# A two-layer hybrid block on one core: output weights split during the projections and kept in DRAM

## The chip, the cores and the metric

The kernel runs on one core of one Trainium2 chip. The metric is the device time of the program in microseconds. A core has TensorE (PE, its weight loads PEld), VectorE (DVE), ScalarE (ACT), GpSimd (POOL), and SyncE (SP), which here issues all DMAs. Each engine runs its own queue of instructions in order.

## What is computed

Two layers over 2048 tokens of width 1024 and 256 context tokens, in float32. The core of a layer, cut from the reference:

```
hx = rmsnorm(x, g_pre) * (1 + scale[:, None]) + shift[:, None]
q, k, v, ga, uf, gf, zc, bc, cc, gc = split_cols(hx @ w_in, PROJ_SIZES)
...
a = window_attention(q, k, v, kc, vc, sink_b)
f = fourier_mix(uf, w_fourier)
s = short_conv_mix(zc, bc, cc, conv_w, conv_b)
y = gated_merge(a, ga, f, gf, s, gc, w_out)
x_new = x + gate[:, None] * rmsnorm(y, g_post)
```

`gated_merge` concatenates `a * silu(ga)` (512 wide), `f * silu(gf)` (256) and `s * silu(gc)` (256) and multiplies by `w_out`, 1024 x 1024 per layer. The context tokens go through the same layer with the context attending to itself; the second layer computes only their keys and values.

## The kernel before

**Number format.** Each float32 operand of a product is split into a high part (rounded to the matmul's format, `fp32r`) and a low part (the rest), and a product is three matmuls: high by high, high by low, low by high. `split` (L76) does this: one engine rounds (L79, L81 or L83 for VectorE, ScalarE, GpSimd), one subtracts (L85 or L87). These lines are those of all splits, so the names of the tiles tell them apart.

**Stages of a layer.** First the projections: `half(l, 0)` takes tokens 0 to 1023 and the context, `half(l, 1)` tokens 1024 to 2047, in chunks of 512 tokens. The normalised input of a chunk, `hx0` or `hx1`, is one pair of tiles `big` (high, low), 128 x 8 x 512 each, from a pool of four. One column block of 128 columns times one chunk is `proj` (L304): 24 matmuls into an `acc` of PSUM, three for each k; `tick` (L118) stands behind each k and advances the generators in `fill` by a rate, so that side work is written into the order between matmuls. Weights come as `wr` (512 KB) and are split to `wh`, `wl`. In half 0 the last stages are the convolution projections (J_CV, with a fill of its own) and a pair of attention gates (J_GA 2 and 3, `sg`, stored to `gas` in DRAM). Half 1 begins with the two Fourier gates (`gf`), the K projection and then V (`accb`).

In layer 0 the input of a chunk is read as `xT` (two loads of 1 MB), and `pt_post` (L275) makes the eight k-slices of `hx`: VectorE `ht<-xT` (L288), ScalarE the high part (L289), VectorE the low (L290). Layer 1's modulation is computed on the side, by products on VectorE (L185) with weights `wmt` of 512 KB. In layer 0 the convolution stage of half 0 also carries `tab_gen` (L598): nine pieces of the Fourier table are loaded (`tr`), split on ScalarE and VectorE (`th`) and stored to `ftd` in DRAM.

Then `phase2(l)`, the attention and the output product, over blocks of 128 tokens (in layer 0 the two context blocks first). Each block has two steps, one for each key head. In a step the generators A (scores and softmax of this block: `sp`, `nm`, `pt`, `es`, `rv`), B (transposes `tp` of the probabilities, split to `ph` and `pl`, product with the values into `op`) and C (output product `yp`) are advanced in the order of the letters in a string; in the first three steps C is instead a gate projection left over from half 1 (`lt`). B also loads the block's gates `gat` and Fourier rows `fct`, and rounds the latter into `hfh` and `hfl` on GpSimd. V and W are `wout_gen(l, 0)` and `wout_gen(l, 1)`: each loads four chunks of 512 KB of its half of the output weights and splits each chunk into a pair of `big`, VectorE and ScalarE (in one case GpSimd) by tables WV and WE. V runs in steps 0 and 1, W in steps 2 and 3. `behind` only says after which instructions of an engine's queue they stand. The order on each engine's queue is fixed when the program is built; a scheduler places the instructions, so a DMA that is written early can stand late.

## Time and profile before

| | us |
|---|---|
| median of 3 runs | 2040.29 (2035.42 to 2041.83) |
| profiled execution, time | 2034.59 |
| profiled execution, span | 2032.8 |
| TensorE busy in it | 1967.9 (97%) |
| VectorE, ScalarE, GpSimd busy | 1245.6, 847.7, 746.4 |

The mean granted clock of TensorE is 0.992 of full. The core reads 214.37 MB of HBM and writes 75.38 MB. The attention of layer 0 begins at about 614 us and of layer 1 at about 1600 us. A busy TensorE is not TensorE at its peak, but where it is not busy the end of the program waits. In a window row the columns are the window, its length, then for PE, PEld, DVE, ACT and POOL the busy time with the number of instructions, then the granted clock, the share of the DMA engines, and GB/s. In a timeline row they are start, duration, engine, line, operation, and in brackets how long the engine sat idle before and who released it.

### The profile page before, as it was taken

To read this page: it belongs to the slowest core of one execution; us is meant where nothing else is said; L and a number is where in the kernel's file an instruction comes from. 1 tells how busy PE (TensorE), PEld (TensorE's weight loads), DVE (VectorE), ACT (ScalarE), POOL (GpSimd) and SP (SyncE) were. 2 spreads that over 40 slices of the span, in tenths; PEclk is the share of its full clock that TensorE was granted. 3 is DMA by queue.
4 is the path that set the end of the run, shared out by engine and by line. 5 is a ranking of instruction groups with operands and counts; after the bars stand their busy time and mean duration, and the time that the engine had idled before them with its cause. 6 is when DMAs were issued, how large, how long until landed. Compare 5 with 4: busy or idle time off the path is not lost.

```text
span 2032.8 us, 28494 instructions
## 1 busy us (share of the span) xinstructions
PE 1967.9 (97%) x10232; PEld 1665.3 (82%) x10232; DVE 1245.6 (61%) x2240; ACT 847.7 (42%) x1742; POOL 746.4 (37%) x965
## 2 busy tenths in 40 slices
PE   6999999999999899999999999999999999999998
PEld 2898788797887788888887988889888778888886
DVE  7824674748535677777778424142764377777775
ACT  6532212213224566666666312131222356666663
POOL 4322232215233444444455333242333434444442
PEclk8999999999999999999999999999999999999999
DMA  7684663566566244444333533134655734444321
GB/s 299 225 254 135 195 201 103 184 200 181 169 186 202 90 112 114 114 113 116 126 116 127 179 89 104 63 112 125 179 178 158 206 113 114 116 115 116 105 63 42
DMA packets 187038, 291.63 MB, mean 143 GB/s; under 512 B 15608, under 2 KB 119696, under 8 KB 185872
## 3 DMA queue, kind: packets, MB, share of 16 engines
q1 hardware_dynamic: 186896, 289.80, 46.8%
q8 instruction: 81, 1.33, 0.3%
q14 instruction: 61, 0.50, 0.1%
HBM read 214.37 MB, written 75.38 MB: 143 GB/s over the span
## 4 chain that ended last, share of the span: by engine, by line
PE 76%; DVE 8%; DMA 7%; POOL 4%; issue 3%; ACT 2%; SPq 1%; DVEq 0%; POOLq 0%; ACTq 0%
PE acc L302 10%; PE acc L300 10%; PE acc L301 10%; PE tp L1159 7%; PE yp L1210 6%; PE yp L1208 6%; PE yp L1209 6%; PE sp L1111 4%; PE op L1173 4%; PE op L1172 3%; PE sp L1108 3%; PE accb L398 2%; PE accb L399 2%; PE accb L400 2%; DMA wmt<-in_wmodt 2%
## 5 line engine op out<-in xcount | busy, mean ns | idle before, releaser
L300 PE MATMUL acc<-big,wh 128*128 128x512 f32 x1152 | 454.9, 395 | 1.6 <-ACT wh L81 1.6
L302 PE MATMUL acc<-big,wl 128*128 128x512 f32 x1152 | 451.0, 391 | 1.9 <-DVE wl L85 1.9
L301 PE MATMUL acc<-big,wh 128*128 128x512 f32 x1152 | 450.7, 391 | 0.6 <-DVE big L290 0.6
L87 POOL TENSOR_TENSOR wl<-wr,wh 128x1024 fp32r<-128x1024 f32 x63 | 158.0, 2508 | 384.5 <-ACT wh L81 275.5
L85 DVE TENSOR_TENSOR pl<-tp,ph 128x512 fp32r<-128x512 f32 x320 | 218.9, 687 | 104.8 <-ACT ph L81 100.4
L1121 ACT ACTIVATE pt<-pt,nm 128x640 f32<-128x640 f32 (+2 forms) x272 | 216.3, 795 | 130.5 <-DVE nm L1118 130.0
L302 PEld LDWEIGHTS acc<-big,wl 128*128 128x128 f32 x1152 | 217.3, 189 | 48.4 <-DVE wl L85 2.8
L300 PEld LDWEIGHTS acc<-big,wh 128*128 128x128 f32 x1152 | 217.7, 189 | 43.9 <-ACT wh L81 2.0
L301 PEld LDWEIGHTS acc<-big,wh 128*128 128x128 f32 x1152 | 217.6, 189 | 43.4 <-DVE big L290 1.0
L81 ACT ACTIVATE ph<-tp 128x512 fp32r<-128x512 f32 x320 | 188.7, 592 | 132.0 <-PE tp L1159 122.5
L1118 DVE CUSTOM_DVE_ANT_0 pt<-sp,mask,nsink 128x640 f32<-128x640 f32 (+2 forms) x256 | 213.3, 841 | 19.8 <-PE sp L1108 14.1
L1133 POOL TENSOR_SCALAR pt<-pt,rv 128x640 f32<-128x640 f32 (+2 forms) x272 | 212.1, 799 | 27.0 <-DVE rv L1131 25.8
L1159 PE MATMUL tp<-ident,pt 128*128 128x128 f32 x1280 | 195.5, 273 | 9.2 <-POOL pt L1133 8.5
L1159 PEld LDWEIGHTS tp<-ident,pt 128*128 128x128 f32 x1280 | 158.9, 140 | 55.4 <-POOL pt L1133 14.1
L1111 PE MATMUL sp<-kseg,qt 128*128 128x384 f32 (+1 forms) x512 | 128.5, 331 | 0.0
L345 POOL TENSOR_TENSOR rs<-rs,sinT 128x512 f32<-128x512 f32 x40 | 67.2, 1682 | 161.1 <-DVE rs L343 156.3
L1208 PE MATMUL yp<-big,hfh 128*128 128x512 f32 x272 | 118.5, 435 | 1.0 <-POOL hfh L83 1.0
L1126 POOL TENSOR_TENSOR es<-nm,nsink 128x4 f32<-128x4 f32 x68 | 14.5, 213 | 282.8 <-DVE nm L1118 282.8
L1208 PE MATMUL yp<-big,hah 128*128 128x512 f32 x272 | 117.1, 431 | 0.1
L1108 PE MATMUL sp<-kctx,qt 128*128 128x256 f32 x544 | 113.9, 291 | 2.9 <-DVE nm L1118 2.1
L1108 PEld LDWEIGHTS sp<-kctx,qt 128*128 128x128 f32 x544 | 95.4, 189 | 16.5 <-DVE nm L1118 3.6
L1210 PE MATMUL yp<-big,hfl 128*128 128x512 f32 x272 | 107.8, 396 | 0.5 <-POOL hfl L87 0.4
(380 smaller groups left out, 3805.4 us busy)
## 6 DMA issues: line engine op xcount, KB each, us to landing
wr<-in_wina SPq DMA_DIRECT2D x76, 512.0 KB, 3.7
qt<-qs SPq DMA_DIRECT2D x34, 512.0 KB, 4.7
wmt<-in_wmodt SPq DMA_DIRECT2D x32, 512.0 KB, 4.3
ftb<-ftd SPq DMA_DIRECT2D x36, 384.0 KB, 4.1
xt<-in_x SPq DMA_DIRECT2D x26, 512.0 KB, 5.9
kseg<-ks SPq DMA_DIRECT2D x24, 512.0 KB, 8.4
xt<-x SPq DMA_DIRECT2D x24, 512.0 KB, 4.5
gat<-gas SPq DMA_DIRECT2D x34, 256.0 KB, 3.1
```

The costliest lines, as they stand in the source:

```text
L85: self.last_v = nc.vector.tensor_tensor(lo, src, f(hi), op=ALU.subtract)
L300: nc.tensor.matmul(a, wh[:, k, :], hi[:, k, :n], start=(k == 0), stop=False)
L301: nc.tensor.matmul(a, wh[:, k, :], lo[:, k, :n], start=False, stop=False)
L302: nc.tensor.matmul(a, wl[:, k, :], hi[:, k, :n], start=False, stop=(k == KT - 1))
L1108: nc.tensor.matmul(sp[:, 256:512], B.q[:, h, :], self.kctx[:, kv, x, :], start=(x == 0), stop=(x == 1))
L1111: nc.tensor.matmul(sp[:, 512:512 + nl], B.q[:, h, :], B.seg[:, kv, x, B.k0:B.k0 + nl], start=(x == 0), stop=(x == 1))
L1118: self.last_m = nc.vector.tensor_tensor_reduce(d, x, m, scale=-0.125, scalar=self.nsink[:, h:h + 1], op0=ALU.add, op1=ALU.min, accum_out=n ...
L1121: self.last_x = nc.scalar.activation(pt, pt, AF.Exp, bias=nm[:, hh:hh + 1], scale=-1.0, accum_out=sm[:, hh:hh + 1])
L1133: self.last_p = nc.gpsimd.tensor_scalar(B.pts[kv][g], B.pts[kv][g], rv[:, g:g + 1], 1.0, op0=ALU.mult, op1=ALU.mult)
L1159: nc.tensor.transpose(tp[:, hh * 128:(hh + 1) * 128], pts[hh][:, t * 128:(t + 1) * 128], self.ident)
L1208: nc.tensor.matmul(yp, hh, wh[:, k, :], start=(i == 0), stop=False)
L1210: nc.tensor.matmul(yp, hl, wh[:, k, :], start=False, stop=(i == KT - 1))
```

## The change

Three things change.

1. `wout_split(l)` is new. It runs in the fill of the convolution stage of half 0, in both layers (in layer 0 behind `tab_gen`). For each of 16 pieces it loads 128 x 512 raw output weights (256 KB), rounds them on ScalarE, subtracts on VectorE, and stores both parts (512 KB) to a DRAM tensor `wos[l]`. The rate of this fill goes from 0.12 to 0.27 in layer 0 and is 0.26 in layer 1.
2. `wout_gen` issues only loads: eight of 512 KB for each half of the weights, high and low parts straight into `big`. The splits in the attention are gone. The strings of steps 2 and 3 place W differently; step 3 has one string for both layers.
3. For the first block of a layer the Fourier rows are rounded behind the last key tile of its second step in place of the second.

The layout of the input `wout` follows. The code before `half` loses five lines, so L85 becomes L80, L190 becomes L185, and so on.

```diff
-WE_A = ["vv", "av", "vv", "av"]
-WE_B = ["vv", "vp", "vv", "av"]
-WV_A = ["vv", "av", "vv", "vv"]
-WV_B = ["vv", "av", "vv", "av"]
-ORDER_2 = "bAACACACWCCBCBCWBCBABBCBBB"
-ORDER_3A = "bAAWCCBcBCABBAWCBBCBBCcACBCBB"
-ORDER_3B = "bAAWCCBcBCABBAWCBBCBBCcACBCBB"
+ORDER_2 = "bAACACACCCBCBCBCBABBCBBB"
+ORDER_3 = "bWAAWCCBcBCABBAWCBBCBBCcACBWCBB"
...
-RT = 0.6, 0.594, 0.616, 0.1, 0.13, 0.12, 0.49
+RT = 0.6, 0.594, 0.616, 0.1, 0.13, (0.27, 0.26), 0.49
...
     def tab_gen(self, p):
         nc = self.nc
         for k in range(9):
-            raw = p.tile([128, 384], F32, name="tr", tag="tr")
+            raw = p.tile([128, CH], F32, name="tr", tag="tr")[:, :384]
             nc.sync.dma_start(raw, self.I["ftab"][:, k])
             yield
-            h = p.tile([128, 2, 384], F32R, name="th", tag="th")
+            h = p.tile([128, 2, CH], F32R, name="th", tag="th")[:, :, :384]
             self.split(h[:, 0], h[:, 1], raw, "a", "v")
             nc.sync.dma_start(self.ftd[k], f(h))
             yield
...
             if half == 0:
                 cvp = self.pool(e3, f"cv{l}{half}", bufs=1)
             fills = [ff] if half else []
-            if l == 0 and half == 0:
-                mp = self.pool(e3, "mp", bufs=1)
-                fills.append(self.start_fill(self.tab_gen(mp), RT[5]))
+            if half == 0:
+                mp = self.pool(e3, f"mp{l}", bufs=1)
+
+                def rest():
+                    if l == 0:
+                        yield from self.tab_gen(mp)
+                    yield from self.wout_split(l, mp)
+                fills.append(self.start_fill(rest(), RT[5][l]))
             for ct in range(2):
                 segs = [("m", HALF), ("c", NCTX)] if (half == 0 and not last_l) else [("m", HALF)]
                 tl = {}
...
             end = t == nkt - 1
             nc.tensor.matmul(op, vv, hl[t][0], start=(t == 0), stop=False)
             nc.tensor.matmul(op, vv, hl[t][1], start=False, stop=end)
-            if kv == 1 and t == 1:
+            if kv == 1 and t == (1 if B is not self.Bs[0] else nkt - 1):
                 B.hf = (p.tile([128, 4, 128], F32R, name="hfh", tag="hfh", bufs=1),
                         p.tile([128, 4, 128], F32R, name="hfl", tag="hfl", bufs=1))
                 self.split(*B.hf, B.fc, "p", "p")
...
         return self.vtiles[b]
 
     def wout_gen(self, l, n):
-        wh, wl = self.big(), self.big()
-        self.wout.append((wh, wl))
-        for c in range(4):
+        W = [self.big(), self.big()]
+        self.wout.append(W)
+        for c in (2, 3, 0, 1):
             with self.behind(self.last_st):
-                raw = self.wraw(self.I["wout"][l, n * 4 + c])
-            sl = slice(c * 128, (c + 1) * 128)
-            with self.behind(self.last_x, self.last_m):
-                self.split(wh[:, :, sl], wl[:, :, sl], raw, *((WV_A, WE_A), (WV_B, WE_B))[l][n][c])
+                for t, src in zip(W, self.wos[l][n]):
+                    self.nc.sync.dma_start(f(t[:, 2 * c:2 * c + 2]), src[:, 2 * c:2 * c + 2])
             yield
+
+    def wout_split(self, l, p):
+        nc = self.nc
+        for n in range(2):
+            for k in range(KT):
+                raw = p.tile([128, CH], F32, name="tr", tag="tr")
+                nc.sync.dma_start(raw, self.I["wout"][l, n, :, k])
+                yield
+                h = p.tile([128, 2, CH], F32R, name="th", tag="th")
+                self.split(h[:, 0], h[:, 1], raw, "a", "v")
+                nc.sync.dma_start(self.wos[l][n, :, :, k].rearrange("x p c -> p x c"), f(h))
+                yield
 
     def ctx_gen(self, l, before):
         nc = self.nc
...
                         drain(V)
                         W = self.wout_gen(l, 1)
                     gens["V"], gens["W"] = V, W
-                    emit(gens, (ORDER_0, ORDER_1, ORDER_2, (ORDER_3A, ORDER_3B)[l])[s])
+                    emit(gens, (ORDER_0, ORDER_1, ORDER_2, ORDER_3)[s])
                     if s == 3:
                         drain(W)
                 else:
...
             c1 = dp.tile([NCTX, D], F32, name="c1")
             self.x = [I["x"], x1, self.out]
             self.ctx = [I["ctx"], c1]
+            self.wos = [dp.tile([2, 2, 128, KT, CH], F32, name=f"wos{l}") for l in range(DEPTH)]
             self.gsl = [dp.tile([128, 2, TOK], F32, name=f"gs_{l}") for l in range(DEPTH)]
             for l in range(DEPTH):
                 self.qs = dp.tile([128, 8, TOK], F32, name=f"qs{l}")
...
     a["winb"] = ac(w_in[:, :, np.r_[640:768, 1280:1536]]).reshape(DEPTH, KT, 128, 384)
     rows = np.concatenate(pairs + [np.arange(512, 1024)])
     wo = w_out[:, rows, :]
-    a["wout"] = ac(wo.reshape(DEPTH, KT, 128, 8, 128).transpose(0, 3, 2, 1, 4)).reshape(DEPTH, 8, 128, KT * 128)
+    a["wout"] = ac(wo.reshape(DEPTH, KT, 128, 2, CH).transpose(0, 3, 2, 1, 4))
     a["sink"] = ac(sink)
     wf = np.zeros((DEPTH, 2, 128, 128), np.float32)
     for g in range(4):
```

The first place is the queue of SP in layer 0, from the end of half 0's convolution stage. `gas<-sg` are the stores of the gates, `xT` the input of half 1's second chunk, `wmt` the modulation weights of layer 1, `tr`, `th` and `wos` the load, the split tile and the store of a piece. Before:

```order
L373 DMA fs_88<-cy 128x256
L783 DMA gas_87<-sg 128x512
L266 DMA xT_3045<-in_xT 128x4x512
L266 DMA xT_3046<-in_xT 128x4x512
L190 DMA wmt<-in_wmodt 128x1024
L783 DMA gas_87<-sg 128x512 x2
```

After:

```order
L1274 DMA wos_81<-th 128x2x512
L1270 DMA tr<-in_wout 128x512
L778 DMA gas_89<-sg 128x512
L778 DMA gas_89<-sg 128x256
L377 DMA wr<-in_winb 128x2x384
L1274 DMA wos_81<-th 128x2x512
L185 DMA wmt<-in_wmodt 128x1024 x2
L261 DMA xT_3143<-in_xT 128x4x512
L261 DMA xT_3144<-in_xT 128x4x512
```

`xT` stood behind the first of the six gate stores; it now stands behind all six, the last store of a piece and two `wmt`.

The second is VectorE right after it, in layer 0, where the second chunk's `hx1` is made; `ISA jk,mo` are products for layer 1's modulation. Before:

```order
L185 ISA jk,mo_1511<-wmt,sb 128x1024
L185 ISA mo_1511 128x1
L181 TENSOR_SCALAR G_1512<-mo_1511,gp_1507 128x2
L185 ISA jk,mo_1511<-wmt,sb 128x1024
L185 ISA mo_1511 128x1
L288 SCALAR_TENSOR_TENSOR ht<-xT_3045,G_153,rb_3049 128x512 x2
L180 TENSOR_SCALAR mo_1511<-mo_1511,bm_1505 128x2
L290 SCALAR_TENSOR_TENSOR big<-ht,mo_152,big 128x512
```

After:

```order
L80 TENSOR_TENSOR th<-tr,th 128x512
L180 ISA jk,mo_1513<-wmt,sb 128x1024
L180 ISA mo_1513 128x1
L180 ISA jk,mo_1513<-wmt,sb 128x1024
L180 ISA mo_1513 128x1
L175 TENSOR_SCALAR mo_1513<-mo_1513,bm_1507 128x2
L180 ISA jk,mo_1513<-wmt,sb 128x1024
L180 ISA mo_1513 128x1
L176 TENSOR_SCALAR G_1514<-mo_1513,gp_1509 128x2
L180 ISA jk,mo_1513<-wmt,sb 128x1024
L180 ISA mo_1513 128x1
L283 SCALAR_TENSOR_TENSOR ht<-xT_3143,G_155,rb_3147 128x512
```

Between the last piece and the first `ht` stand four such products now, and five more among the `ht` and `big` that follow.

The third is GpSimd at the start of layer 0's attention, with `-` for before and `+` for after:

```order
 L1133 TENSOR_SCALAR pt<-pt,rv 128x256 x4
-L87 TENSOR_TENSOR hfl<-fct,hfh 128x512
 L1126 TENSOR_TENSOR es<-nm,nsink 128x4
 L1128 TENSOR_TENSOR es<-es,sm 128x4
 L1133 TENSOR_SCALAR pt<-pt,rv 128x256 x4
+L78 TENSOR_SCALAR hfh<-fct 128x512
+L82 TENSOR_TENSOR hfl<-fct,hfh 128x512
```

`hfh` stood ahead of the first of these `pt`. Both roundings stand behind the second group now.

## Rows read from the trace of the kernel before

**Rows 1.** The page, busy time of each engine.

```profile
PE 1967.9 (97%) x10232; PEld 1665.3 (82%) x10232; DVE 1245.6 (61%) x2240; ACT 847.7 (42%) x1742; POOL 746.4 (37%) x965
```

**Rows 2.** Windows of the attention's starts, of half 0, and of two half-clock stretches.

```profile
core 0: us, PE busy (x) PEld busy (x) DVE busy (x) ACT busy (x) POOL busy (x), PEclk, DMA share, GB/s
614.00:670.00 56.00, 49.73 (x239) 38.47 (x238) 33.91 (x72) 26.71 (x65) 17.23 (x28) 1.00 0.56 184
670.00:720.00 50.00, 47.46 (x259) 39.45 (x259) 35.35 (x70) 27.53 (x65) 23.34 (x43) 1.00 0.40 116
720.00:816.00 96.00, 96.00 (x538) 82.29 (x538) 73.68 (x140) 58.74 (x132) 41.46 (x82) 1.00 0.41 112
1594.00:1710.00 116.00, 108.57 (x576) 90.06 (x575) 81.81 (x147) 63.50 (x138) 43.93 (x69) 0.99 0.50 144
235.00:290.00 55.00, 50.31 (x246) 42.56 (x245) 43.40 (x74) 9.85 (x18) 13.21 (x6) 0.94 0.71 233
290.00:345.00 55.00, 55.00 (x295) 47.60 (x294) 24.18 (x41) 7.44 (x13) 17.20 (x7) 1.00 0.25 87
239.70:246.60 6.90, 5.91 (x15) 4.66 (x16) 4.19 (x13) 1.74 (x3) 1.53 (x1) 0.51 0.70 263
1656.30:1659.70 3.40, 3.40 (x11) 2.82 (x10) 2.15 (x5) 3.21 (x6) 0.00 (x0) 0.50 0.02 5
```

**Rows 3.** TensorE's waits, 614 to 705 us, then 1594 to 1662 us.

```profile
PE tp L1159 <- POOL pt L1133: 5.6, 7, 1.7
...
PE op L1173 <- DVE pl L85: 2.8, 2, 2.2
```

**Rows 4.** Groups by line and form, VectorE, 614 to 672 us.

```profile
L85 DVE TENSOR_TENSOR big<-wr,big 128x1024 fp32r<-128x1024 f32 x8 | 10.2, 1284 | 0.2
```

**Rows 5.** Timeline of VectorE, layer 1's start.

```profile
1635.01 1.21 DVE L85 TENSOR_TENSOR big<-wr,big 128x1024 fp32r<-128x1024 f32 x1
...
1638.93 1.27 DVE L85 TENSOR_TENSOR pl<-tp,ph 128x512 fp32r<-128x512 f32 x2
```

**Rows 6.** Timeline of GpSimd, layer 0's start.

```profile
631.79 3.74 POOL L1133 TENSOR_SCALAR pt<-pt,rv 128x256 f32<-128x256 f32 x4
635.50 2.24 POOL L87 TENSOR_TENSOR hfl<-fct,hfh 128x512 fp32r<-128x512 f32 x1
...
639.53 2.33 POOL L1133 TENSOR_SCALAR pt<-pt,rv 128x256 f32<-128x256 f32 x4 [1.12 <-DVE rv L1131]
```

**Rows 7.** The page, costliest groups: the splits of a 128 x 512 tile.

```profile
L85 DVE TENSOR_TENSOR pl<-tp,ph 128x512 fp32r<-128x512 f32 x320 | 218.9, 687 | 104.8 <-ACT ph L81 100.4
...
L81 ACT ACTIVATE ph<-tp 128x512 fp32r<-128x512 f32 x320 | 188.7, 592 | 132.0 <-PE tp L1159 122.5
```

**Rows 8.** The tile `tr`, 190 to 300 us.

```profile
L81 ACT ACTIVATE th<-tr x8: 513/525/527, 230.1 to 282.4; 128x384 fp32r<-128x384 f32 x8
...
DMA to landing us min/median/max: 2.7/3.1/5.2
```

**Rows 9.** The tile `xT`, 340 to 400 us.

```profile
L288 DVE SCALAR_TENSOR_TENSOR ht<-xT,G,rb x8: 734/740/742, 369.6 to 382.7; 128x512 f32<-128x512 f32 x8
L266 SPq DMA_DIRECT2D xT<-in_xT x2: 384/442/500, 347.0 to 347.4; - x2
...
DMA to landing us min/median/max: 6.8/8.4/9.9
```

**Rows 10.** DMA issues, 340 to 400 us.

```profile
wmt<-in_wmodt SPq DMA_DIRECT2D x6, 512.0 KB, 4.2
```

**Rows 11.** Timeline of TensorE, start of half 1.

```profile
365.80 0.39 PE L300 MATMUL acc<-big,wh 128*128 128x512 f32 x1
...
385.39 0.50 PE L301 MATMUL acc<-big,wh 128*128 128x512 f32 x1 [0.58 <-DVE big L290]
...
402.29 0.34 PE L398 MATMUL accb<-wbh,big 128*128 128x384 f32 x1
```

**Rows 12.** Timeline of VectorE, start of half 1.

```profile
367.19 1.21 DVE L185 CUSTOM_DVE_ANT_0 jk<-wmt,sb 128x1024 bf16<-128x1024 f32 x1
```

## Prediction

> **What bounds the kernel now.** I read the page first: of a 2032.8 us span TensorE is busy 1967.9 us, 97% [rows 1]. No other engine passes 62%, so time can come only from the 65 us in which TensorE is not busy, or from making it wait more. The profiled execution took 2034.59 us, 1.8 us more than its span; the median of the three runs is 2040.29, so I make the sum against 2034.6 and add 5.7 us to carry it to the median.
>
> Next I cut the span into stretches around the places the change touches. The reader is to see that the attention is full in steady state (layer 0, 720 to 816 us: 96.00 of 96) and not at its start: in layer 0 49.73 of 56 us while the weights are split, 47.46 of 50 right after; in layer 1 108.57 of 116, and 3.4 us more at half clock behind the last stall (a granted clock of 0.50, that is 1.2 GHz of 2.4) [rows 2]. So 6.3, 2.5 and 7.4 us of idle TensorE, and 1.7 us of lost clock. This is what the change can give at first hand.
>
> Then the waits. At layer 0's start TensorE waits 5.6 us, in seven pieces, for `pt` of GpSimd; at layer 1's start 2.8 us for `pl` of VectorE [rows 3]. The question is whether the work on the output weights makes these late.
>
> **Part 1, the splits that leave the attention.** In layer 0 VectorE spends 10.2 us on eight subtractions of weights [rows 4], beside five roundings on it and three on ScalarE; layer 1 has much the same. Their cost is not their busy time, since both engines have idle time there, but their place in a queue that runs in order. The timeline of VectorE in layer 1 shows it: the subtraction of a weight stands at 1635.01 us, with its cast before it and `lt` after it, ahead of the `pl` that TensorE waits for, which starts only at 1638.93 [rows 5]. That is the longest wait, 2.2 us, of the 2.8. The same queue order stands behind the late row maxima and, through them, behind the late `pt`.
>
> **Part 2, the rounding of the first block's Fourier rows.** On GpSimd `hfh` waits for its load with `pt` behind it; then `hfl` takes 2.24 us and the next block's sums stand behind that [rows 6]. The change puts both behind the second group of `pt`, so the next `pt` no longer stand behind a load and two roundings.
>
> A row against a rule: the four `pt` at 631.79 took 3.74 us, and the four at 639.53 took 2.33 [rows 6]; beside the first VectorE worked on a subtraction. The Trainium skill (SBUF — State Buffer, Who interferes with whom) says that a VectorE instruction with two inputs in SBUF contends with a GpSimd instruction that reads SBUF. By that rule the 1.4 us come back with the subtractions gone, and the same contention appears in half 0, between the new subtractions and the GpSimd weight splits; the trace agrees as far as these two rows go. Without that rule layer 0 gives 1.4 us less.
>
> What goes: in layer 0 the 6.3 us, less a short wait on a gate's evacuation that stays, so 6; in layer 1 7.4 + 1.7 = 9.1, less the like and a rest of the half clock, so 8: **−14**. Not counted are the 2.5 us of 670 to 720 in layer 0, where no weight is being split any more. Bounds: −18 if all of it goes with them, 6.3 + 2.5 + 7.4 + 1.7; and −5 if only half of the waits of rows 3 (8.4 us) and of the lost clock go, because the next engine is late for the rest. I take −14 since a split, or `hfl`, stands ahead of the late instruction in each gap I followed back.
>
> **Part 3, the loads in the attention.** Four MB of raw weights per layer become eight MB, in sixteen loads of 512 KB. The busiest stretch of the rows moves 263 GB/s [rows 2]; 8 MB at that rate are 32 us, and the half that the first output product reads (4 MB, loaded first) 16 us, 25 with the other loads between them. That product starts near 655 us, some forty after the loads. SP issues five of them ahead of `gat` and `fct`, so `fct` lands some 10 us later; its rounding has been put later too. I cost this at 0, with up to 4 us if `fct` or the next `qt` is late: the upper bound of what the wait for `fct` could put back.
>
> **Part 4, the splits and stores in half 0.** Sixteen pieces per layer: a 256 KB load, a rounding on ScalarE, a subtraction on VectorE, a 512 KB store. A tile of this shape takes ScalarE 592 ns and VectorE 687 [rows 7]. The narrower pieces of the table, with loads of 3.1 us, run in the same way now, eight of them from 230 to 283 us, and TensorE waits for none [rows 8]. Busy time: 16 × 1.3 = 20 us per layer on two engines that from 290 to 345 us are busy 24.18 and 7.44 of 55 us while TensorE is full [rows 2]. Cost 0, bound +3.
>
> **Part 5, what the pieces push back.** The 9 + 16 pieces of layer 0 fill the whole convolution stage and run into the gate projections behind it. On SP the load of the next half's second chunk (`xT`, two of 1 MB) now stands behind the last store and two `wmt` loads. Before, it was issued at 347.0 and landed in 6.8 to 9.9 us, a good 12 us ahead of its first use at 369.6; the last tile was ready at 385.3, and TensorE already waited for it there [rows 9, 11]. This cover is used up. I place the issue: the store of the last context gate, whose projection ends where the next begins, at 365.8, precedes it [rows 11], with five more DMAs at some 0.4 us each, so 368.5. The two `wmt` land 4.2 us later, and four modulation products of 1.2 us stand ahead on VectorE [rows 10, 12]: 377.5; `xT` lands at 375 to 378. From there eight `ht` and eight `big` of 0.74 and five products, 18 us, to 395.5. TensorE, which goes through both Fourier-gate projections in step with these tiles, has then one k of them and two K projections left. From the wait at 385.39 to `accb` at 402.29 there are 74 matmuls, 0.228 us each [rows 11]; 48 for K and 6 for the last k are 12.3 us: 408, against 402.3. So **+6**. Bounds: 0, if the tiles come no later than now, and +12, if the last piece waits for its own load and store one after the other and `xT` is issued at 373.
>
> **Sum:** −14 + 6 + 0 + 0 = −8: 2034.6 → 2026.6 profiled, **2032** as a median. 0.3%, about what a measurement of this kernel can tell from no change, is 6.1 us.
>
> **The rivals.**
>
> *The starts stay as they are.* The 2.5 us of 670 to 720 have no split beside them, so a start may stall because its blocks change size, with another engine late in its turn. Then the attention gives −5, half 1 takes 6: 2036 profiled, 2041 on the median. For it: those stalls exist. Against: the timeline of rows 5.
>
> *The chain of pieces becomes the bound (slower).* Load, ScalarE, VectorE and store have one buffer each, and the order on each engine is fixed, so a late piece holds up the evacuations and weight splits behind it. From 230 to 365 us there are 135 us; nine narrow pieces of at most 0.5 + 0.7 + 3.1 us and 0.4 to issue, 4.7 in all, leave 93 for sixteen wide ones, 5.8 us each. My estimate of a wide cycle, from the rows of tile and load, is 0.6 + 0.7 + 3.1 + 0.5 = 4.9 us. It decides from 6 us: a table load took up to 5.2 us, with 233 GB/s moved in 235 to 290 [rows 2, 8]. At 7 us the last store comes 19 us late (16 × 1.2) and everything of part 5 with it: −14 + 6 + 19 = +11, so 2046 profiled, 2051 as a median.
>
> *No cost in half 1.* If `xT` is early enough, the whole −14 stands: 2020.6 profiled, 2026 on the median. Against it stands the order on SP.
>
> *The clock falls in the new wait.* TensorE would run in step with the tiles for some 18 us at little over half its work. At 239.7 to 246.6 us, after a long wait, the granted clock was 0.51 of full, that is 1.2 GHz, for 6.9 us [rows 2]: 3.4 us of work lost. The Trainium skill (TensorE: Matmul & The Clock Gate, HAM oscillation — how this bites in real kernels) describes a clock that falls again in each gap between bursts. By that rule the K projections would start at half clock and the loss be 6 + 3.4: −4.6, 2030 profiled, 2036 as a median. The trace bears out one fall after one long wait, and one of 3.4 us in layer 1's start.
>
> *The change does not do what it says.* The order of instructions shows splits and roundings moved, so I give this nothing.
>
> **How the numbers follow.** Forecast (net −5 to −12) 0.43; no cost in half 1 0.12; clock 0.15; the starts stay 0.18; chain the bound 0.12. Of the forecast's cases about three quarters lie beyond −6.1, of the clock's a third, and all of the third rival: faster 0.5. The starts-stay case and the rest of the forecast and clock give same 0.37. The chain, and a little of the starts-stay case with 12 us in half 1, give slower 0.13. The range reaches from −18 with nothing given back (2022), and a little below for the spread of the runs, to +6 (2046), which leaves out the worse half of the chain: 2020 to 2046.
>
> **What would show it.** Right: no wait for `pl` or `pt` behind a `big` at the starts, TensorE busy about 55 of 56 and 115 of 116 us in the two stretches; `xT` issued about 368 and the first `accb` of half 1 about 408. Wrong: stalls of the same sum at both starts with another releaser; the first `accb` at 402 or past 415; waits of ScalarE on `tr` that TensorE shares in half 0.

## The result, and the profile after

The changed kernel is slower by 0.6%: a median of 2052.1 us (2049.31 to 2053.13, 4 runs) against 2039.74 for the kernel before on the same chip, a ratio of 1.006 [1.0041, 1.008]. The profiled execution took 2053.13 us, its span is 2051.3, 18.5 longer than before. The medians differ by 12.4 only: the profiled execution of the kernel before lies 5.2 us under its median, this one 1.0 above. The page's first row:

```profile
PE 1974.7 (96%) x10232; PEld 1670.6 (81%) x10232; DVE 1246.2 (61%) x2247; ACT 859.8 (42%) x1768; POOL 731.8 (36%) x964
```

TensorE has the same number of matmuls as before [rows 1]. Of the 18.5 us 6.8 are longer busy time in them, and 11.7 are waiting. To find where, I set the start of the same matmul in both traces side by side:

| before, us | after is later by | what lies in between |
|---|---|---|
| 87 | 1.7 | the start, which the change does not touch: clock |
| 327 | 1.5 | |
| 350 | 12.9 | layer 0, half 0, convolution stage |
| 388 | 27.0 | first Fourier-gate projections of half 1 |
| 408 | 33.5 | the rest of them, into the K projections |
| 610 | 33.5 | |
| 670 to 1050 | 24.8 | start of layer 0's attention: −8.7 |
| 1455 | 25.8 | layer 1's half 0 |
| 1500 to 1600 | 29.5 | layer 1's Fourier transform |
| 1676 to the end | 18.5 | start of layer 1's attention: −11.0 |

So the attention gave more than forecast (−19.7), and layer 0's projections took back 32. The windows of the changed kernel (window, its length, busy time and count of each engine, granted clock, DMA share, GB/s):

```profile
core 0: us, PE busy (x) PEld busy (x) DVE busy (x) ACT busy (x) POOL busy (x), PEclk, DMA share, GB/s
647.50:694.80 47.30, 46.78 (x239) 38.92 (x239) 21.18 (x60) 23.36 (x62) 12.73 (x28) 1.00 0.80 268
694.80:744.80 50.00, 47.59 (x259) 39.30 (x259) 35.37 (x70) 27.53 (x65) 23.36 (x43) 1.00 0.51 152
1623.50:1728.50 105.00, 104.74 (x576) 89.08 (x575) 67.51 (x135) 60.94 (x135) 36.92 (x68) 1.00 0.68 199
352.00:360.00 8.00, 5.39 (x13) 4.23 (x14) 6.85 (x10) 1.12 (x2) 3.24 (x2) 0.50 0.64 202
380.00:404.00 24.00, 12.22 (x50) 9.63 (x51) 14.48 (x27) 5.90 (x10) 0.63 (x1) 0.79 0.81 283
```

The first three hold the same matmuls as three of [rows 2]. The 239 of layer 0's start took 56.0 us and now take 47.3; the 576 of layer 1's took 116 and now take 105. The 259 of 670 to 720 still take 50, with 2.4 us idle in place of 2.5. The last two are the new losses. TensorE's waits there (us in total, times, longest), 300 to 440 us, and then the one for `pt` at layer 0's attention, 645 to 740 us (5.6 us in [rows 3]):

```profile
PE acc L295 <- ACT big L284: 11.5, 2, 11.1
PE acc L295 <- ACT wh L76: 5.0, 2, 4.5
PE acc L297 <- POOL wl L82: 4.8, 2, 3.5
PE accb L394 <- POOL wbl L82: 2.2, 2, 1.8
...
PE tp L1159 <- POOL pt L1133: 1.6, 3, 0.7
```

**The first stall, 345 to 355 us.** Three timelines tell it, in order of time. SyncE, whose queue issues the DMAs (start, time to issue):

```profile
335.51 0.38 SPq L1274 DMA_DIRECT2D wos<-th  x1
335.94 0.46 SPq L1270 DMA_DIRECT2D tr<-in_wout  x1
...
342.27 0.38 SPq L1274 DMA_DIRECT2D wos<-th  x1
342.70 0.46 SPq L185 DMA_DIRECT2D wmt<-in_wmodt  x1
343.26 0.79 SPq L1270 DMA_DIRECT2D tr<-in_wout  x1
```

ScalarE (in brackets how long it sat idle, and for whom):

```profile
340.89 0.63 ACT L76 ACTIVATE th<-tr 128x512 fp32r<-128x512 f32 x1 [5.46 <-DMA tr<-in_wout]
...
347.82 0.63 ACT L76 ACTIVATE th<-tr 128x512 fp32r<-128x512 f32 x1 [5.81 <-DMA tr<-in_wout]
348.36 0.58 ACT L979 ACTIVATE czm<-acc 128x512 f32<-128x512 f32 x1
348.83 1.05 ACT L76 ACTIVATE wh<-wr 128x1024 fp32r<-128x1024 f32 x1
```

TensorE, then GpSimd and VectorE in the same stretch:

```profile
349.93 0.80 PE L295 MATMUL acc<-big,wh 128*128 128x512 f32 x1 [4.47 <-ACT wh L76]
...
354.61 0.79 PE L297 MATMUL acc<-big,wl 128*128 128x512 f32 x1 [3.45 <-POOL wl L82]
...
349.01 2.80 POOL L349 TENSOR_TENSOR cbm<-cbm,czm 128x1024 f32<-128x1024 f32 x1 [11.28 <-ACT czm L979]
351.77 2.79 POOL L82 TENSOR_TENSOR wl<-wr,wh 128x1024 fp32r<-128x1024 f32 x1
...
349.53 2.83 DVE L80 TENSOR_TENSOR th<-tr,th 128x512 fp32r<-128x512 f32 x1
352.28 2.30 DVE L175 TENSOR_SCALAR mo<-mo,bm 128x2 f32<-128x2 f32 x1
```

One late piece explains both waits. The load for it is issued only after the store of the piece before (342.27) and after one `wmt`. ScalarE stands at its `th` for 5.81 us, with the evacuation `czm` and the weight cast `wh` behind it; TensorE lacks `wh` for 4.47 us. GpSimd could not begin `cbm` without `czm`, and `wl` stands behind `cbm`: 3.45 us more. Inside the first of the two waits, at 349.7, TensorE's granted clock falls to 0.50, that is 1.2 GHz, and it stays there until 359.9.

**The second stall, 388 to 408 us.** SyncE and ScalarE, then TensorE:

```profile
389.09 0.45 SPq L1274 DMA_DIRECT2D wos<-th  x1
389.59 1.77 SPq L185 DMA_DIRECT2D wmt<-in_wmodt  x2
391.46 2.81 SPq L261 DMA_DIRECT2D xT<-in_xT  x2
...
393.95 0.59 ACT L272 COPY rb<-prb 128x512 f32<-128x512 f32 x1 [5.28 <-DMA wos<-th]
...
402.50 1.22 PE L295 MATMUL acc<-big,wh 128*128 128x512 f32 x2 [11.10 <-ACT big L284]
```

The last piece is stored at 389.09; before, the last table piece was stored at 283.6. The load of `xT` comes behind it, at 391.46 instead of 347.0 [rows 9]. `rb`, a tile that the same stage needs, waits for that store too: its memory is the pieces'. TensorE waits 11.1 us, and its clock falls again in this wait.

**The pieces.** Sixteen stores of layer 0 go out from 281.1 to 389.1 us, 15 intervals of 7.2 on average (5.7 to 10.1). The prediction had counted room for one every 5.8 us. The issues (count, KB each, median us to landing), 190 to 400 us, and what ScalarE and VectorE wait for there (ScalarE 190 to 402, VectorE 300 to 422 us):

```profile
wos<-th SPq DMA_DIRECT2D x16, 512.0 KB, 3.1
tr<-in_wout SPq DMA_DIRECT2D x16, 256.0 KB, 4.2
...
ACT th L76 <- DMA tr<-in_wout: 80.3, 16, 8.5
...
DVE jk L180 <- DMA wmt<-in_wmodt: 21.4, 5, 7.2
DVE th L80 <- ACT th L76: 17.6, 7, 5.1
```

### The profile page after: what moved, and what is told of

The parts are those of the page before. It is cut to its first block, busy times and chain, and to the rows that moved or that the text cites. A ratio compares the mean times of both kernels' runs of the same rounds, so it can differ in the third digit from the quotient of the medians.

```text
span 2051.3 us, 28664 instructions
## 1 busy us (share of the span) xinstructions
PE 1974.7 (96%) x10232; PEld 1670.6 (81%) x10232; DVE 1246.2 (61%) x2247; ACT 859.8 (42%) x1768; POOL 731.8 (36%) x964
## 4 chain that ended last, share of the span: by engine, by line
PE 74%; DVE 10%; DMA 8%; POOL 3%; issue 3%; ACT 2%; SPq 1%; DVEq 0%; POOLq 0%; ACTq 0%
PE acc L297 9%; PE acc L295 9%; PE acc L296 9%; PE tp L1159 7%; PE yp L1208 6%; PE yp L1210 6%; PE yp L1209 6%; PE sp L1111 4%; PE op L1173 4%; PE op L1172 3%; PE sp L1108 3%; DMA wmt<-in_wmodt 3%; PE accb L394 2%; PE accb L395 2%; PE accb L393 2%
## 5 line engine op out<-in xcount | busy, mean ns | idle before, releaser
L80 DVE TENSOR_TENSOR pl<-tp,ph 128x512 fp32r<-128x512 f32 x320 | 219.5, 687 | 109.3 <-ACT ph L76 104.8
L1118 DVE CUSTOM_DVE_ANT_0 pt<-sp,mask,nsink 128x640 f32<-128x640 f32 (+2 forms) x256 | 213.1, 841 | 21.4 <-PE sp L1108 15.1
L1133 POOL TENSOR_SCALAR pt<-pt,rv 128x640 f32<-128x640 f32 (+2 forms) x272 | 207.4, 783 | 25.5 <-DVE rv L1131 24.3
L180 DVE CUSTOM_DVE_ANT_0 jk<-wmt,sb 128x1024 bf16<-128x1024 f32 x56 | 78.8, 1407 | 61.7 <-DMA wmt<-in_wmodt 61.2
```

Source lines behind the costliest of these rows:

```text
L80: self.last_v = nc.vector.tensor_tensor(lo, src, f(hi), op=ALU.subtract)
L1118: self.last_m = nc.vector.tensor_tensor_reduce(d, x, m, scale=-0.125, scalar=self.nsink[:, h:h + 1], op0=ALU.add, op1=ALU.min, accum_out=n ...
L1133: self.last_p = nc.gpsimd.tensor_scalar(B.pts[kv][g], B.pts[kv][g], rv[:, g:g + 1], 1.0, op0=ALU.mult, op1=ALU.mult)
```

## The experiments

My theory was that the sixteen pieces of layer 0 are a chain of latencies (load, ScalarE, VectorE, store, one buffer each) that is slower than the rate at which the order places them, and stands in queues which run in order. The rivals put the loss on the bytes moved, on the memory shared by the pieces with `xT` and `rb`, on the queue that issues the DMAs, or on the modulation products. Times are medians; each ratio is against runs of the kernel before on the same chip.

**1. Which layer, and which part.** The first kernel leaves layer 0's weights as before, the second layer 1's, the third has only the edit for the late rounding of the Fourier rows.

```diff
-                    yield from self.wout_split(l, mp)
+                    if l in NEW:
+                        yield from self.wout_split(l, mp)
...
+        if l not in NEW:
+            for c in range(4):
+                with self.behind(self.last_st):
+                    raw = self.wraw(self.I["woutc"][l, n * 4 + c])
```

(`NEW` holds the layers with pieces; the lines of `wout_gen` bring back the raw chunks and their splits. A layer without pieces has the strings of before, and layer 0 without them the rate of 0.12.)

> Layer 0 works as before the change, with its output weights split in the attention (the later rounding of the first Fourier rows stays in both layers); layer 1 has the change. Theory A, the chain: the loss lies in layer 0's 25 pieces, one buffer each, one after the other, in half 0. Then layer 1 shows what the trace of the change shows for it: about 11 us less at its attention's start, about 5 more in its half 0 and Fourier stage, so 6 less than before, 2034. Theory B, the traffic: 4 MB more read and 8 MB more written per layer slow all loads beside them. Then layer 1's half 0 pays like layer 0's, 20 us or more, and the time is above 2045.

> Layer 0 has the change, layer 1 works as before it (but for the later rounding). Theory A: the +32 us around the end of half 0 and the -9 at layer 0's attention stay: 23 more than before, 2063. Theory B: the same sign but about half of the change's loss in each layer, so about 2046.

```diff
-            if kv == 1 and t == 1:
+            if kv == 1 and t == (1 if B is not self.Bs[0] else nkt - 1):
```

> Only the later rounding of the first block's Fourier rows, all else as before the change. If it gives a part of its own: 1 to 3 us, 2037 to 2038.5, in the attention's starts; if the splits hide it, nothing.

Measured: layer 1 alone 2030.8 us, 0.9955 [0.9943, 0.9968]; layer 0 alone 2062.24, 1.011 [1.0084, 1.0135]; the third 2038.11, 0.9997 [0.9981, 1.0013]. The layers add up: −8.7 and +22.8 make +14, the change +12.4. Layer 0 alone has the change's stalls at the same places. The third run moved no rounding. In layer 0 the first block is a context block with two key tiles, so that the last tile is the second; and in the traces GpSimd has the same instructions in the same order as before through the whole program, layer 1 included. So the third item of the change does nothing by itself, this kernel is the one before once more, and what a later rounding is worth was not measured. Where the roundings stand behind both groups of `pt` in the changed kernel's layer 0, this comes with its other edits.

The run still holds a row: with the weights split in the attention, the first four `pt` took as long as the 3.74 us of [rows 6]; in the changed kernel, with neither weight subtractions on VectorE nor the roundings at either side, they are short. GpSimd, first of this run, then of the change:

```profile
632.25 1.66 POOL L83 TENSOR_SCALAR hfh<-fct 128x512 fp32r<-128x512 f32 x1 [2.29 <-DMA fct<-fs]
633.89 3.73 POOL L1133 TENSOR_SCALAR pt<-pt,rv 128x256 f32<-128x256 f32 x4
637.59 1.28 POOL L87 TENSOR_TENSOR hfl<-fct,hfh 128x512 fp32r<-128x512 f32 x1
```

```profile
664.64 2.28 POOL L1133 TENSOR_SCALAR pt<-pt,rv 128x256 f32<-128x256 f32 x4 [2.05 <-DVE rv L1131]
...
667.91 1.85 POOL L1133 TENSOR_SCALAR pt<-pt,rv 128x256 f32<-128x256 f32 x4 [0.31 <-DVE rv L1131]
```

**2. The floor.** Two pieces per layer instead of sixteen; the attention loads them over and over, so most of the output weights are missing. The rate in layer 0 is 0.13.

```diff
-        for n in range(2):
-            for k in range(KT):
+        for n in range(1):
+            for k in range(2):
...
-                for t, src in zip(W, self.wos[l][n]):
+                for t, src in zip(W, self.wos[l][0]):
```

> The change with 2 of the 16 pieces per layer; the attention's 16 loads of each layer read those two pieces again and again, so their number and bytes stay (14 pieces are left out, so most of the output weights are missing). It gives the attention's gain by itself. Theory A: no cost in half 0, xT on time, all of the 9 + 11 us at the attention's starts: 2018 to 2023. Rival: if the 8 MB of loads or the start itself cost something that half 0's delay hid, less than 14 us are gained, 2026 or more.

Measured: 2022.64, 0.9919 [0.9894, 0.9944]; TensorE's longest wait from 300 to 440 us is 1.2 us. The attention gains 8.8 and 11.1 us in the trace, with the same sixteen loads of 512 KB per layer, and TensorE waits 0.8 us in all for one of them. The pieces cost 1.006 − 0.9919, 1.4% or 29 us.

**3. The order of load and store.** The next load is issued ahead of the store.

```diff
                 nc.sync.dma_start(raw, self.I["wout"][l, n, :, k])
+                if st:
+                    nc.sync.dma_start(*st)
...
-                nc.sync.dma_start(self.wos[l][n, :, :, k].rearrange("x p c -> p x c"), f(h))
+                st = self.wos[l][n, :, :, k].rearrange("x p c -> p x c"), f(h)
```

> The change with one swap: the next piece's load is issued ahead of the store of the piece before, not behind it; bytes and work are the same. Theory A: the load no longer stands behind 512 KB on the rings and lands in about 3.1 us in place of 4.2, a piece takes about 5.2 us in place of 6.3 and more, the last store goes out near 370 us in place of 389, and the cost in layer 0 falls from 32 us to 8 to 15: 2028 to 2036. Theory B: same bytes, same cost: 2050. Theory C, the input xT alone is late and the blocked queues cost nothing: the gain is only the part of 22 us by which xT comes earlier, 2035 to 2045.

Measured: 2048.07, 1.0041 [1.0023, 1.0058]. This missed the 2028 to 2036 that the chain theory set, and lies nearer to the 2050 of the traffic. The load is early now and lands in 3.0 us by the median in place of 4.2, but `th` has one buffer, and ScalarE waits for the store instead:

```profile
ACT th L76 <- DMA wos<-th: 62.9, 13, 6.9
```

The stores go out 6.2 us apart on average (5.6 to 7.7), the last at 373.1, 16 us earlier, but `xT` still only at 379 and 383.6, behind two `wmt`. A chain with one buffer at each end has a second wait right behind the first.

**4. No wait for the load.** Layer 0's pieces split a table that lies in memory, so its output weights are wrong; the loads and stores stay.

```diff
-                self.split(h[:, 0], h[:, 1], raw, "a", "v")
+                self.split(h[:, 0], h[:, 1], raw if l else src, "a", "v")
```

> The change, but layer 0's pieces split a table that lies in SBUF in place of the loaded weights (so layer 0's output weights are wrong); the loads and stores are issued with the same bytes, and nothing on ScalarE or VectorE waits for such a load. Theory A: the stalls of TensorE between 340 and 356 us go, the pieces are through before 350, xT comes on time: 25 us or more of the 32 are regained, 2025 to 2031. Theory B (the traffic of 4 + 8 MB): the loss stays, 2045 or more.

Measured: 2045.29, 1.0025 [1.0009, 1.0041]. A miss again: 2025 to 2031 was expected, and 2045 or more was the mark of the traffic. By the trace another wait took the place of the first: ScalarE waits for the store of the piece before 14 times, 72.1 us in all (3.1 to 8.1), and TensorE lacks `wh` for 6.5 us until 356. The time alone does not part this from the traffic.

**5. The memory.** The pieces' pool is opened ahead of the convolution's, so that `xT` and `rb` fall on other buffers.

```diff
             if half == 0:
+                mp = self.pool(e3, f"mp{l}", bufs=1)
                 cvp = self.pool(e3, f"cv{l}{half}", bufs=1)
...
-                mp = self.pool(e3, f"mp{l}", bufs=1)
```

> The change with one line moved: the memory of the pieces is taken before that of the convolution tiles, so xT, the next half's input, no longer lies on top of the pieces' buffers and its load stands ahead of the last four stores. Theory C (xT, late behind the last store, costs most): the 11 us wait for hx1 and the half clock behind it go, the first 11.5 us (345 to 355) stay: 15 to 20 us less than the change, 2033 to 2037. Theory A alone (the waits of ScalarE for the pieces' loads cost, xT only follows): 5 us less at most, 2047.

> The change with both the load first and the memory of the pieces taken first. If their parts add up (4 and 11.5 us): 2036. If both only move the same wait: 2040.

Measured: 2040.61, 1.0007 [0.9993, 1.0021], 11 us better than the change, and between the two times expected. The loads of `xT` go out at 363 and 369, and the wait of 11.1 us is gone; that of the first stall is as before:

```profile
PE acc L295 <- ACT wh L76: 5.3, 2, 4.3
PE acc L297 <- POOL wl L82: 3.9, 2, 3.4
```

So the shared memory is a third of the loss, and not the rest: set beside the kernel before as in the first table, this kernel is later by 13.4 us at 350, about as the change, but by 19.6 at 436, in place of 33.6. The bytes are the same, so bytes alone do not make the loss. Together with the load issued first: 2046.54, 1.0042 [1.0028, 1.0057], above both times expected. The two do not add up, and why they are slower together than the second alone stays open.

**6. The DMAs alone.** Layer 0 makes two real pieces; fourteen more only load a tile and store it, without ScalarE and VectorE.

```diff
+            for k in range(14):
+                raw = p.tile([128, CH], F32, name="tr", tag="tr")
+                nc.sync.dma_start(raw, self.I["wout"][l, k // 8, :, k % 8])
+                yield
+                nc.sync.dma_start(self.dum[k], raw.rearrange("p (u c) -> p u c", u=1).broadcast_to([128, 2, CH]))
```

> Layer 0: two real pieces, then fourteen that are only loaded and stored twice over from the loaded tile, 256 KB in and 512 KB out like a piece, each store behind its load on SP, with nothing on ScalarE and VectorE; the attention reads the two real pieces again and again (so most output weights are missing in both layers, and layer 1 has two pieces too). Theory A' (the loss is the waits of the pieces on the two compute engines' queues): 2022 to 2028, as with two pieces (2022.6). Theory D (the head of SP's queue): wmt and xT late, 2034 or more. Theory B (the bytes): 2040 or more.

Measured: 2039.21, 0.9989 [0.9979, 1.0], which is 0.7% or 14 us above the floor. VectorE's and TensorE's waits, from 300 us:

```profile
DVE jk L180 <- DMA wmt<-in_wmodt: 45.8, 8, 10.4
...
PE acc L295 <- ACT big L284: 9.1, 2, 7.9
PE acc L295 <- ACT wh L76: 4.8, 2, 4.3
```

VectorE waited 6.6 us for `wmt` in the kernel before. Each store here waits for its load at the head of SyncE's queue, and the `wmt` loads behind it, which need nothing from it, wait too. `xT` goes out at 383.6, behind the last store; but its memory is the pieces' here as well. So half the loss comes without the splits, and this run does not part the queue's share of it from the memory's. Its place can be told: set beside the kernel before, this kernel is later by 0.2 us at 350 and by 22.3 at 436 (the change 12.9 and 33.6). The DMAs alone bring the loss at the start of half 1, and nothing of the stall of 345 to 355, for all of VectorE's waits. The other half, 0.7% again, comes with the splits on ScalarE and VectorE (a few us of it are layer 1's pieces).

**7. Other queues.** The pieces' DMAs are issued by GpSimd, or by ScalarE, or the pieces are split by GpSimd (and the projection weights of that stage by ScalarE and VectorE alone).

```diff
-                nc.sync.dma_start(raw, self.I["wout"][l, n, :, k])
+                (nc.sync if l else nc.gpsimd).dma_start(raw, self.I["wout"][l, n, :, k])
```

> The change, but layer 0's pieces are loaded and stored by GpSimd's queue in place of SP's; bytes, buffers, ScalarE's and VectorE's work stay. Theory D (SP's queue: a store that waits for VectorE and a load that waits for a buffer hold up the wmt and xT loads behind them, so products pile up in the gate stage, which is full): wmt and xT come as before the change, 15 us or more are regained, 2036 or less; what the waits of ScalarE cost near 345 to 356 (11 us) stays. Theory B (traffic): 2048 or more. A risk: GpSimd's weight splits stand behind the stores' waits in its queue.

> The change with layer 0's 16 pieces loaded and stored from ScalarE's queue. Theory D: wmt free, so about 15 us of the 32 go; what the chain does to ScalarE and VectorE stays, some 10 to 17 us with the last store ahead of xT: 2034 to 2042. If ScalarE's added waits weigh as much as SP's: 2050.

```diff
-                self.split(h[:, 0], h[:, 1], raw, "a", "v")
+                self.split(h[:, 0], h[:, 1], raw, *("av" if l else "pp"))
```

> The change, but layer 0's pieces are rounded and subtracted by GpSimd, and the projection weights of that stage are split by ScalarE and VectorE alone, so that no weight stands behind a piece. Theory A': TensorE no longer waits for evacuations or weights between 340 and 356; what remains is xT behind the last store: 2030 to 2040. Theory D or B: 2047 or more.

Measured: 2052.56, 1.0066 [1.0045, 1.0086]; 2050.71, 1.0061 [1.0039, 1.0083]; 2055.74, 1.0066 [1.0044, 1.0088]. The first and the third are misses (2036 or less and 2030 to 2040 by my theory), the second is the worse of its two cases. The first two free VectorE of its waits for `wmt` (2.8 and 3.0 us now, 21.4 in the change), with all the bytes still moved: the delay of `wmt` is a place in a queue and not bandwidth. But the wait goes with the DMAs. TensorE's waits on GpSimd's queue, then on ScalarE's:

```profile
PE acc L297 <- POOL wl L82: 14.1, 5, 4.4
```

```profile
PE acc L297 <- POOL wl L82: 6.8, 4, 2.6
PE acc L295 <- ACT wh L76: 5.5, 1, 5.5
```

With the pieces split on GpSimd, VectorE takes over weight splits and stands 10.57 us at a product for its `wmt`, with `wl` behind it:

```profile
348.13 1.23 DVE L180 CUSTOM_DVE_ANT_0 jk<-wmt,sb 128x1024 bf16<-128x1024 f32 x1 [10.57 <-DMA wmt<-in_wmodt]
```

```profile
363.60 0.79 PE L297 MATMUL acc<-big,wl 128*128 128x512 f32 x1 [16.94 <-DVE wl L80]
```

**8. Half the pieces.** Layer 0 makes the pieces of one half of its output weights, and splits the other half in the attention: the first half, then the second, then the second with its DMAs on ScalarE's queue. (For the second half, `n == 0`; `ns` is the half that is made. The rate in layer 0 is 0.19.)

```diff
+        if l not in NEW and n == 1:
...
-        for n in range(2):
+        for n in ns:
```

> Layer 1 as in the change; in layer 0 only the first half of the output weights (8 pieces) goes through half 0, the second half is split in the attention as before. Theory A: 9 + 8 pieces end before the gates, xT stands early, no loss in half 0; of layer 0's 9 us in the attention about half come: 2026 to 2029, a little below the run with layer 1 alone (2030.8). If a chain of 17 costs too, 2032 or more.

> Layer 1 as in the change; in layer 0 only the second half of the output weights (8 pieces) goes through half 0, the first is split in steps 0 and 1 of the attention as before. The stalls of the attention that the change removed lay at 638 to 665 us, steps 2 and 3, where the second half is split: 5 to 7 us gained there. If half 0 costs the 10 us of the run with the first half (x7): 2034 to 2036; if that cost was chance: 2026.

> x15 (layer 1 as in the change, in layer 0 only the second half of the output weights through half 0), with layer 0's pieces loaded and stored from ScalarE's queue. Theory D: wmt and xT come as before the change, the 5.2 us wait near 380 and the rest of the 9 us lost in half 0 go, the 5 us of layer 0's attention stay: 2024 to 2028. If ScalarE's waits for the store's tile and the load's buffer cost as much: 2032 or more.

Measured: 2039.72, 0.9993 [0.9976, 1.0009]; 2032.01, 0.9954 [0.9936, 0.9971]; 2033.01, 0.9975 [0.9961, 0.9988]. Eight pieces cost 9.8 and 9.5 us ahead of layer 0's attention in the first two, 6.1 and 5.3 of it at the start of half 1 (365 to 388). The first half's pieces bring 1.4 us in layer 0's attention, the second half's 6.1: the start stalls mostly where W's splits stand, not V's. On ScalarE's queue, where 2024 to 2028 was hoped for, a new wait comes:

```profile
PE acc L302 <- DVE cTm L982: 5.8, 1, 5.8
```

**9. Products earlier.** The rate of the modulation products is raised, in the change, in layer 1 alone, and in the second half.

```diff
-RT = 0.6, 0.594, 0.616, 0.1, 0.13, (0.27, 0.26), 0.49
+RT = 0.6, 0.594, 0.616, 0.1, 0.17, (0.27, 0.26), 0.49
```

> The change with the rate of layer 1's modulation products raised from 0.13 to 0.17: 52 of 56 products stand ahead of the second chunk's input in VectorE's order, 42 in the change. Theory D: 10 products of 1.2 us less in the full gate stage, 5 to 10 us less than the change: 2042 to 2047. If only the pieces' own waits cost: 2050 or more.

> Layer 1 with the change, layer 0 without, and the rate of the modulation products 0.17 as above (56 of 56 ahead of the second chunk's input, 44 without). If VectorE is what TensorE waits for in the gate stage and at half 1's start (3 us of stalls): 2028; if the products cost as much where they are now: 2031.

> x15 with the modulation products at rate 0.17, so that nearly all of them stand ahead of the second chunk's input and VectorE no longer waits for a wmt load in the gate stage (it sat idle 8 us for one in x7). If that wait made x7's loss: 2026 to 2029, the best of all with correct weights; if not, as x15 or slower.

Measured: 2062.56, 1.0115 [1.0097, 1.0133]; 2030.69, 0.996 [0.9945, 0.9974]; 2038.76, 0.9988 [0.9974, 1.0003]. The first and the third are misses. In the first, 42 instead of 32 of the 56 products come before 345 us, but the pieces wait for them: the last split of a piece ends at 400.6.

**The best version** is layer 1 alone, 2030.8 us (8 runs), 0.45% below the kernel before; the second half's pieces with layer 1's are as fast within the intervals. Both beat both kernels.

## Why the prediction was wrong

**Parts 1 and 2, the attention: right in mechanism, too small.** Forecast −14, measured −19.7: −8.7 against −6 in layer 0, −11.0 against −8 in layer 1. The stalls went as read, and the idle 2.5 us of 670 to 720 stayed (2.4 now), as I assumed when I left them out. How much of it is part 2's, no run shows. What the term lacked is hidden in the busy share. In layer 0 the same 239 matmuls were busy 49.73 us [rows 2] and are now busy 46.78; in layer 1 576 were busy 108.57 and are now 104.74. So a stretch with stalls loses 3.0 and 3.8 us more in matmuls that count as busy; half a clock explains 1.7 of the 3.8. I had summed idle time alone.

The row against a rule came out for the rule: the first four `pt` fell from 3.74 to 2.28 us and the next from 2.33 to 1.85, once no subtraction of a weight ran beside them, and the first stayed at 3.73 where those were kept. The Trainium skill (SBUF — State Buffer, Who interferes with whom) says that VectorE and GpSimd share one pair of ports, which one holds to the exclusion of the other; these rows agree.

**Part 3, the loads in the attention:** 0 forecast. TensorE waits 0.6 us for a `big` from `wos`. Right.

**Part 4, the pieces: here the prediction failed.** "TensorE waits for none" of the narrow pieces and "Cost 0, bound +3" did not carry over. The estimate of a wide cycle was 0.6 + 0.7 + 3.1 + 0.5 = 4.9 us. Measured: the load lands in 4.2 us in place of 3.1, and 4.2 + 0.63 + 0.68 + 0.4 + 0.4 is 6.3 before anything is in its way; with `wmt` loads and products in the way it was 7.2 on average. Two things were missing: the 3.1 us was that of loads of 192 KB, while a load of 256 KB right behind a store of 512 KB takes 4.2 (3.0 ahead of it, experiment 3); and the piece was costed alone though its four instructions stand in three queues with other work. That 20 us of work on engines that are mostly idle can be hidden says nothing of 16 waits of 5 us each on the same engines (ScalarE's 80.3 us). This was the second rival, "the chain of pieces becomes the bound": it set the point at 6 us a piece and 2051 us as the price at 7. Measured were 7.2 and 2052.1. The price agrees partly by luck: it charged all of it to `xT` and none to stalls inside half 0 (11.4 us of the 32), and its +25 and −14 miss +32 and −19.7 by about as much. The sign that the prediction had named for being wrong, waits of ScalarE on `tr` that TensorE shares in half 0, is the stall of 345 to 355. The chance of 0.12 was too low: its own condition lay 1.1 us above an estimate made from the best case.

**Part 5, the late `xT`:** right mechanism, wrong size. "I place the issue ... so 368.5" was 391.46, since it took the last piece to be done at 365.8. The cost in half 1 was 20.6 us and not 6. The last `accb` starts at 469.6 instead of 436.0, 33.6 later. The first, at 421.1, doesn't compare: in the new order it stands ahead of part of the K projections. That `rb` and `xT` lie on the pieces' memory, worth 11 us by experiment 5, was not in the prediction at all.

**What the runs part.** The 20.6 us at the start of half 1 need no splits (experiment 6) and fall to 6.2 when `xT` lies on other memory than the pieces (5). The 11.4 us of half 0 need the splits (6), but neither an earlier load (3) nor no wait for the load (4) takes them away, since the wait for the store stands right behind. That single buffers are the cause there is therefore argued from the waits; no run took both waits away.

**The clock rival** came true inside the chain, and twice: 0.50 from 349.7 us, in the wait of 4.47, and from 394.1, in that of 11.1, with matmuls 0.43 us apart in place of 0.23.

```profile
349.70:359.90 10.20, 6.51 (x15) 4.63 (x16) 9.05 (x10) 2.05 (x5) 5.54 (x3) 0.50 0.50 155
394.10:407.70 13.60, 5.20 (x11) 3.46 (x12) 11.65 (x22) 3.76 (x6) 0.00 (x0) 0.50 0.99 364
```

The 546 matmuls of 327 to 436 us before (328.4 to 469.6 now) were busy 106.1 us and are now busy 115.9. So some 10 of the 32 us are longer matmuls and 22 are waits; the prediction priced the clock at 3.4. The Trainium skill (TensorE: Matmul & The Clock Gate, HAM oscillation — how this bites in real kernels) describes such a fall in a gap; these rows agree.

**Left over.** Of the 4.7 us that layer 1 lost ahead of its attention, 1.7 is a wait for `wl` in the stage with the pieces. The rest is a wait for VectorE in the Fourier transform and the clock behind it, which layer 1 alone does not show. It is not layer 1's pieces: layer 0 alone has it too, with 3.3 us; its cause stays open. Two buffers for each piece, the direct test of the chain, were not tried. Nor was the whole traffic run with no waits at all, so that the share of the bytes in the longer landing times stays open.

## What to carry to other kernels

Side work that loads, computes and stores through single buffers has a latency per piece; set that, measured among the other transfers, against the rate at which the order places the pieces, and not its busy time against idle engines. Where it is the slower, every queue that carries a part of it holds up what stands behind, and moving it to another queue moves the wait. And where a pool is closed, look at who gets its memory: the last store of the side work may release a load of the main path.

## What was not expected of the hardware

A subtraction of 128 x 512 on VectorE, 0.69 us in fifteen of the sixteen pieces, took 2.83 us where it ran beside GpSimd's `cbm` (349.01 to 351.81), and a VectorE instruction on 128 x 2 took 2.30 us and ended at 354.58, beside `wl`, which ended at 354.56. GpSimd's `wl` itself lasted 2.79. So the contention reaches both ways: in the attention the subtractions of weights slowed GpSimd's `pt`, here GpSimd held VectorE in the middle of the stall.

A load of 256 KB that was issued right behind a store of 512 KB on the same queue landed in 4.2 us by the median (3.6 to 6.0). Issued ahead of the store, with the same bytes, it landed in 3.0 (2.9 to 5.1, experiment 3); one of 192 KB in the kernel before in 3.1 [rows 8].
